# Causal masking on GpSimd instead of TensorE, the second softmax division on GpSimd, and a few instructions issued at other places

## The chip, the cores and the metric

The program runs on 1 core of one Trainium2 chip, in one launch. The metric is the device time in microseconds (us), the median of several runs: 1357.43 us for the kernel before (3 runs, 1357.02 to 1357.74). The engines of the core are TensorE (PE in the profile), VectorE (DVE), ScalarE (ACT), GpSimd (POOL) and SyncE (SP), each of which works through its own list of instructions in order; they wait for one another on semaphores.

## The reference

A trunk of two layers works on 512 tokens of 1024 features in float32, with 16 heads of 64 features.

```
layer 0:  hn = rms_norm(h) * g;  q, k, v = hn @ W_qkv
          z = q.k / 8 ;  strict: key < query
          w = sigmoid(z) * prod over later keys of (1 - sigmoid(z))     # stick-breaking weights
layer 1:  k, v, f from rms_norm(h) @ W_kvf, q from rms_norm(h) @ W_q;  k, q with a norm per head
          z = q.k / 8 + F[query] - F[key],  F = cumsum(log_sigmoid(f + b))
          w = softmax(z) over key <= query                              # forgetting attention
each:     h += (w @ v) @ W_o
          h += (silu(hn2 @ W_g) * (hn2 @ W_u)) @ W_d                    # 22 tiles of 128 hidden features
          h += sigmoid(rms_norm(h) @ W_gate) * (p[layer] @ W_proj)
```

## The kernel before, in words

Everything lies transposed: features on the 128 partitions, the 512 tokens as columns. So h is eight tiles h[0..7] of 128x512, and a norm's factor per token has to be spread over the partitions: `norm_spread` (L255 on) does it with four small matmuls of plain float32 (L258), and ScalarE copies the result `rb` to SBUF.

Each float32 operand of a product is split into a high part in the type fp32r and a low remainder, and a product is three matmuls: high by high, high by low, low by high (`mm3`, L274 to L276; `by_token`, L431 to L434, for q, k and v). The weights come in "units" of 128x1024 by DMA on SP's queue. ScalarE rounds a unit to its high part `wh` (L154 for the first units, L171 and L175 later), and VectorE subtracts to get `wl` (L139).

The attention of a layer goes head by head. `qk` makes the projections of two heads; `expand` and `put` turn them into `qd`, `kd` and `ke` (kd and ke exchange halves by DMAs on GpSimd's queue, L561). `front(hd)` has three score tiles, each in a PSUM bank `z`: tile 0 holds the block j=0 of 128 tokens against 512 columns, tile 1 the block j=1 against 384, tile 2 the block j=3 against 128 and the block j=2 against 256. `scores` issues two matmuls for a block (L635 with ke, L636 with kd). For block j=3 before computes 256 columns and uses the last 128 of them. In layer 1 `hide` then adds a mask to the diagonal block of 128 columns by a third matmul (L643) with `identb` and a bfloat16 mask; in tile 2 one such matmul of 256 columns serves both blocks. In layer 0 the sigmoids are computed with no mask and GpSimd's affine_select (L680) sets the forbidden weights to zero.

After the scores, layer 1 does for each tile: VectorE adds the head's row of gate sums `gb` (brought from DRAM by a GpSimd DMA, L656) and takes the minimum in one instruction (L695), ScalarE takes the exponential with the sum beside it (L699), VectorE the reciprocal (L701), and ScalarE multiplies the weights by it (L703). Layer 0 uses sigmoids (L677), a scan (L684) and a multiplication (L687).

`back(hd)` turns the weights on TensorE (transposes, L736, into `pt`), ScalarE and VectorE split them (L737, L139), and TensorE multiplies them with v (L744). After the second head of a pair, at L764 to L772, VectorE and ScalarE make from the result the operands `bh` and `bl` of the output projection.

What stands between these steps on TensorE is a pump (`Filler`, table `STEPS`): matmuls of later projections, of later v, and in the end of `first_part` (eight tiles of the first half of W_o, 12 matmuls each) are handed out in small numbers between the steps of the heads, so that TensorE has work while a head's weights are computed on the other engines. Behind the last head the second half of W_o follows; three of its tiles are begun (9 matmuls each) before the ones that need the last pair of heads. A scheduler places the instructions at build time and so fixes each engine's list; `pin` forces a given order there.

The end of the kernel is the gate of layer 1: per tile VectorE computes `s` (L359), adds it to h (L360) and SP stores h (L362).

Of the kernel before, what the change touches and what calls it, by code (L numbers as in the profile page):

```python
# [24 lines left out]
P = 128  # L25
# [19 lines left out]
I32 = mybir.dt.int32  # L45
BF16 = mybir.dt.bfloat16

# [38 lines left out]
def trunk(ctx, tc, xT, pT, small, wf, wall, out, dump=None):  # L86
# [29 lines left out]
    make_identity(nc, ident)  # L116


    identb = const.tile([P, P], BF16, name="identb")
    nc.vector.tensor_copy(identb, ident)  # L120
    masks = []
    for i, (op, fill) in enumerate(((ALU.is_gt, -1.0e30), (ALU.is_ge, 1.0e30))):
        mf = tp.tile([P, S], F32, name="mf", tag="ta")
        nc.gpsimd.memset(mf[:, :P], 0.0)
        nc.gpsimd.affine_select(out=mf[:, :P], in_=mf[:, :P], pattern=[[1, P]], compare_op=op,
                                fill=fill, base=0, channel_multiplier=-1)
        mb = const.tile([P, P], BF16, name=f"mask{i}")
        nc.vector.tensor_copy(mb, mf[:, :P])
        masks.append(mb)
    one = const.tile([P, 1], F32, name="one")  # L130
# [16 lines left out]
    def load_half(u, i):  # L147

        if i == 0:
            units[u] = tuple(wpool.tile([P, 1024], F32R, name=f"w{x}{u}", tag=f"w{x}", bufs=WBUFS)  # L150
                             for x in "hl")
        wh, wl = units[u]
        c = slice(i * 512, i * 512 + 512)
        nc.scalar.copy(wh[:, c], raws[u][:, c])  # L154
        minus(wl[:, c], raws[u][:, c], wh[:, c])
        if i == 1:
            raws.pop(u)
            state["unit"] = u + 1
# [59 lines left out]
    def add_square(k, c0=0, cn=S):  # L218
        c = slice(c0, c0 + cn)
        if k == 0:  # L220
            nc.scalar.activation(acc[:, c], h[k][:, c], AF.Square)
        else:
            sq = tp.tile([P, S], F32, name="sq", tag="ta")
            nc.scalar.activation(sq[:, :cn], h[k][:, c], AF.Square)
            nc.vector.tensor_tensor(acc[:, c], acc[:, c], sq[:, :cn], ALU.add)
# [45 lines left out]

    def mm3(ps, wblk, xh, xl, first, last):
        wh, wl = wblk
        nc.tensor.matmul(ps, wh, xh, start=first, stop=False)  # L274
        nc.tensor.matmul(ps, wh, xl, start=False, stop=False)  # L275
        nc.tensor.matmul(ps, wl, xh, start=False, stop=last)  # L276
# [21 lines left out]
    def ffn(layer, buf, g_next):  # L298
        last = layer == 1
        with tc.tile_pool(name=f"pf{layer}", bufs=8, space=PSUM, reuse_waits="tile") as ppool["d"], \  # L300
# [54 lines left out]
            def close_gate(n, s, pp):  # L355
                cn = S // len(pp)
                for c0, ps in pp:
                    c = slice(c0, c0 + cn)
                    nc.vector.tensor_tensor(s[:, c], s[:, c], ps[:, :cn], ALU.mult)  # L359
                    nc.vector.tensor_tensor(h[n][:, c], h[n][:, c], s[:, c], ALU.add)  # L360
                    if last:
                        nc.sync.dma_start(out[:, n * S + c0:n * S + c0 + cn], h[n][:, c])  # L362
                    else:
                        emit_x(n, 1 - buf, g_next, True, c0, cn)
# [33 lines left out]
    def attention(layer, buf):  # L398
        stick = layer == 0
        mask = masks[layer]  # L400
        xs = operand(buf)
        with tc.tile_pool(name=f"pa{layer}", bufs=1, space=PSUM, reuse_waits="tile") as pa, \
# [67 lines left out]
            if stick:  # L470
# [10 lines left out]
                run(v0)  # L481
                rb = norm_spread(r, pz, "z")
            oh, ol = bh[1 - buf], bl[1 - buf]
# [146 lines left out]

            def scores(zt, c, n, d, j, s0, first=True, done=stick):
# [4 lines left out]
                nc.tensor.matmul(zt[:, c:c + n], qd[:, t], kd[:, s0:s0 + n], start=False, stop=done)  # L636

            def hide(zd):

                if stick:  # L640
                    return
                m = mask.unsqueeze(1).to_broadcast([P, zd.shape[1] // P, P])
                nc.tensor.matmul(zd, identb, m, start=False, stop=True)  # L643


# [4 lines left out]
            def front(hd):  # L650
# [3 lines left out]
                if not stick:  # L654
                    gb = a2.tile([P, S], F32, name="gb", tag="gb")
                    nc.gpsimd.dma_start(gb, gdram[hd:hd + 1, :].to_broadcast([P, S]))  # L656
                for ti, segs in enumerate(TILES):
                    n = sum(sg[2] for sg in segs)
                    z = pz.tile([P, S], F32, name="z", tag="z")
                    if ti == 2:  # L660

                        scores(z, 0, 256, d, 3, 256, True, False)
                        scores(z, 256, 256, d, 2, 256, False)
                        z = z[:, P:]
                        hide(z[:, :2 * P])
                    else:
                        scores(z, 0, n, d, segs[0][0], segs[0][0] * P)
                        z = z[:, :n]
                        hide(z[:, :P])
                    w = a2.tile([P, S], F32, name="w", tag="w", bufs=WB[layer])  # L670
# [18 lines left out]
                    else:  # L689
# [4 lines left out]
                        for si, (j, c, m) in enumerate(segs):  # L694
                            nc.vector.tensor_tensor_reduce(  # L695
                                w[:, c:c + m], z[:, c:c + m], gb[:, j * P:], 1.0, 3.0e38,
                                ALU.add, ALU.min, mx[:, si:si + 1])
# [15 lines left out]
            def back(hd):  # L713
# [26 lines left out]
                def product(gi, low):  # L740
                    blks, th, tl, uses = groups[gi]
                    for s, c, m in uses:
                        vv = v[:, s, hd % 4].rearrange("p a d -> p (a d)")
                        nc.tensor.matmul(po[:, :m], vv, (tl if low else th)[:, c:c + m],  # L744
                                         start=gi == 0 and not low, stop=gi == 2 and low)

# [30 lines left out]
            if stick:  # L777
                run(qk(0))
            else:
# [12 lines left out]
                run(group(0, sums, spread))  # L792
                gdram = tok["g"]
                run(expand(0))
            for e in attn_order(layer)[2:]:
                i = int(e[1:])
                if e == "e7":
                    continue
                fill.add(e, qk(i) if e[0] == "p" else expand(i) if e[0] == "e" else
                         group(i) if e[0] == "g" else values(i, (bank("v"),) if i == 0 else ()))  # L800
# [212 lines left out]
```

## Time and profile before

| | |
|---|---|
| median of 3 runs | 1357.43 us (1357.02 to 1357.74) |
| the profiled execution | 1356.89 us |
| its span, in which the rows stand | 1355.2 us |
| TensorE busy | 1337.9 us (99%), 6236 matmuls |
| VectorE busy | 808.2 us (60%) |
| ScalarE busy | 628.0 us (46%) |
| GpSimd busy | 75.5 us (6%) |
| chain that ended last | 86% on TensorE |

All times in rows are microseconds from the start of the span, unless marked ns. A row of a timeline has the start, the duration, the engine, the line of the kernel, the operation, and output<-inputs with their shapes; in brackets stands how long the engine was idle before it and what ended that. Matmuls overlap in the array: a row's duration is from its issue to its end, and what a matmul costs in a dense stretch is the distance from its start to the next one's, not its duration. PEld is TensorE's weight load, which runs beside the matmul ahead of it.

### The profile page before, as it was taken

How to read it: one execution, taken by the hardware profiler on the slowest of the kernel's cores; microseconds unless marked ns; L12 is line 12 of the kernel's file. 1: busy time of each engine (PE TensorE's matmuls, PEld its weight loads, DVE VectorE, ACT ScalarE, POOL GpSimd, SP SyncE). 2: the span in 40 equal slices, each digit the busy share in tenths (PEclk: the TensorE clock that was granted, in tenths of full speed). 3: DMA queues.
4: the chain of work that ended last, by engine and by line, in shares of the span. 5: the costliest groups of instructions: out<-in, count | busy, mean ns of one | idle time of the engine just before them, and what ended most of it. 6: DMA issues, size and time to landing. Idle time of an engine off the chain costs nothing.

```text
span 1355.2 us, 16550 instructions
## 1 busy us (share of the span) xinstructions
PE 1337.9 (99%) x6236; PEld 1095.2 (81%) x6236; DVE 808.2 (60%) x1388; ACT 628.0 (46%) x1099; POOL 75.5 (6%) x146
## 2 busy tenths in 40 slices
PE   8999999999999999999999999999999999999998
PEld 7788887888888888888877777777888888888887
DVE  6898998754444443334867887787544444434335
ACT  6676776532223332222648788685322322322212
POOL 0221220000000000000010101000000000000000
PEclk9999999999999999999999999999999999999999
DMA  6332331233333233322333433332333323322323
GB/s 203 109 94 63 101 99 66 93 101 94 95 104 96 93 94 100 102 94 70 111 110 94 110 101 102 101 99 81 101 96 105 95 93 95 107 93 94 95 68 109
DMA packets 41856, 133.34 MB, mean 98 GB/s; under 512 B 7456, under 2 KB 7840, under 8 KB 41776
## 3 DMA queue, kind: packets, MB, share of 16 engines
q1 hardware_dynamic: 37248, 119.63, 28.2%
q0 software_dynamic: 4384, 12.62, 3.6%
q8 instruction: 49, 0.80, 0.3%
q14 instruction: 31, 0.25, 0.1%
q10 hardware_dynamic: 144, 0.03, 0.0%
HBM read 121.73 MB, written 2.14 MB: 91 GB/s over the span
## 4 chain that ended last, share of the span: by engine, by line
PE 86%; ACT 4%; issue 4%; DVE 3%; DMA 1%; POOL 1%; SPq 0%; POOLq 0%; DVEq 0%; ACTq 0%
PE ps L275 24%; PE ps L276 24%; PE ps L274 24%; PE pb L431 2%; PE pb L434 2%; PE pb L433 2%; PE po L744 2%; PE pt L736 2%; PE z L635 1%; PE z L636 1%; ACT wh L171 1%; POOL w L680 1%; ACT w L699 1%; DMA raw<-in_w_dram 0%; ACT ke L549 0%
## 5 line engine op out<-in xcount | busy, mean ns | idle before, releaser
L274 PE MATMUL ps<-bh,wh 128*128 128x512 f32 x1216 | 478.1, 394 | 1.9 <-DVE bh L767 1.9
L275 PE MATMUL ps<-bl,wh 128*128 128x512 f32 x1216 | 474.8, 390 | 1.0 <-DVE bl L139 1.0
L276 PE MATMUL ps<-bh,wl 128*128 128x512 f32 x1216 | 474.9, 391 | 0.0
L175 ACT CAST wh<-raw 128x1024 fp32r<-128x1024 f32 x188 | 197.7, 1052 | 484.5 <-PE ps L275 426.0
L139 DVE TENSOR_TENSOR wl<-raw,wh 128x1024 fp32r<-128x1024 f32 (+1 forms) x196 | 235.1, 1200 | 162.9 <-ACT wh L175 161.8
L276 PEld LDWEIGHTS ps<-bh,wl 128*128 128x128 f32 x1216 | 228.3, 188 | 47.7 <-DVE wl L139 0.4
L274 PEld LDWEIGHTS ps<-bh,wh 128*128 128x128 f32 x1216 | 228.3, 188 | 47.1 <-DVE bh L767 2.5
L275 PEld LDWEIGHTS ps<-bl,wh 128*128 128x128 f32 x1216 | 228.5, 188 | 46.2 <-DVE bl L139 2.0
L431 PE MATMUL pb<-wh,bh 128*128 128x512 f32 x256 | 105.8, 413 | 1.9 <-ACT wh L154 1.3
L317 DVE TENSOR_TENSOR s<-s,ps 128x512 f32<-128x512 f32 x44 | 30.2, 687 | 126.9 <-PE ps L276 126.7
L433 PE MATMUL pb<-wl,bh 128*128 128x512 f32 x256 | 101.3, 396 | 0.2 <-DVE wl L139 0.2
L434 PE MATMUL pb<-wh,bl 128*128 128x512 f32 x256 | 100.7, 396 | 0.0
L315 DVE TENSOR_TENSOR s<-ps,rb 128x512 f32<-128x512 f32 x44 | 30.2, 690 | 95.7 <-PE ps L276 79.9
L274 PE MATMUL ps<-eh,wh 128*128 128x512 f32 x224 | 87.2, 389 | 0.0
L276 PE MATMUL ps<-eh,wl 128*128 128x512 f32 x224 | 87.2, 389 | 0.0
L275 PE MATMUL ps<-el,wh 128*128 128x512 f32 x224 | 87.1, 389 | 0.0
L431 PEld LDWEIGHTS pb<-wh,bh 128*128 128x128 f32 x256 | 48.4, 189 | 10.4 <-issue 2.1
L434 PEld LDWEIGHTS pb<-wh,bl 128*128 128x128 f32 x256 | 48.1, 188 | 9.7
L433 PEld LDWEIGHTS pb<-wl,bh 128*128 128x128 f32 x256 | 48.5, 190 | 7.3 <-DVE wl L139 0.5
L736 PE MATMUL pt<-ident,w 128*128 128x128 f32 x320 | 52.9, 273 | 1.3 <-DVE w3l L139 1.3
L684 DVE TENSOR_TENSOR_SCAN e<-e,own 128x512 f32<-128x512 f32 (+1 forms) x64 | 51.5, 826 | 3.1 <-ACT e L677 2.8
L736 PEld LDWEIGHTS pt<-ident,w 128*128 128x128 f32 x320 | 39.7, 140 | 13.2 <-DVE w3l L139 3.1
(177 smaller groups left out, 1572.0 us busy)
## 6 DMA issues: line engine op xcount, KB each, us to landing
raw<-in_w_dram SPq DMA_DIRECT2D x212, 512.0 KB, 3.5
kd<-ke POOLq DMA_DIRECT2D x32, 128.0 KB, 3.3
ke<-kd POOLq DMA_DIRECT2D x32, 128.0 KB, 3.7
gb<-gdram POOLq DMA_DIRECT2D x16, 256.0 KB, 3.5
h<-in_x_dram SPq DMA_DIRECT2D x8, 256.0 KB, 4.4
raw<-in_w_dram SPq DMA_DIRECT2D x8, 256.0 KB, 4.0
out_dram<-h SPq DMA_DIRECT2D x7, 256.0 KB, 2.1
pf<-in_p_dram SPq DMA_DIRECT2D x2, 512.0 KB, 4.6
```

The lines of the kernel that those rows point to most:

```text
L139: nc.vector.tensor_tensor(out, a, b.bitcast(F32), ALU.subtract)
L175: nc.scalar.copy(wh, raw)
L274: nc.tensor.matmul(ps, wh, xh, start=first, stop=False)
L275: nc.tensor.matmul(ps, wh, xl, start=False, stop=False)
L276: nc.tensor.matmul(ps, wl, xh, start=False, stop=last)
L315: nc.vector.tensor_tensor(s, g, rb, ALU.mult)
L317: nc.vector.tensor_tensor(s, s, u, ALU.mult)
L431: pin(nc.tensor.matmul(ps, xh, wh, start=k == 0, stop=False), stick and k == 0)
L433: nc.tensor.matmul(ps, xh, wl, start=False, stop=False)
L434: nc.tensor.matmul(ps, xl, wh, start=False, stop=k == ND - 1)
L684: nc.vector.tensor_tensor_scan(e[:, c:c + m], e[:, c:c + m], own[:, :m], 1.0, ALU.mult, ALU.max)
L736: nc.tensor.transpose(pt[:, bi * P:(bi + 1) * P], blk(j, s), ident)
```

## The change

1. The masks: `identb`, the two mask tiles and `hide`'s matmul go (48 matmuls in layer 1). Instead `gb` gets 128 more columns, and GpSimd writes a large number over the forbidden part of its diagonal block, four affine_selects of 128x128 a head: for block 0 and block 3 (into the added columns) when `gb` has landed, for blocks 1 and 2 when the row has been used by the tile before.
2. The scores of block j=3 are computed with 128 columns, not 256: 64 matmuls in both layers.
3. The multiplication by the reciprocal in layer 1 goes from ScalarE (L703) to GpSimd (64 instructions).
4. `first_part` keeps back its eighth tile; its 12 matmuls come behind the last head's last product and ahead of the late part, in both layers.
5. Order: in layer 0 `norm_spread` comes five steps later in `qk(0)`; the first weight unit's copy comes ahead of the square of h[0] on ScalarE; in layer 1 the first steps of `values(0)` are called before `expand(0)`.
6. In the last gate one residual addition (tile 6) goes from VectorE to GpSimd.

```
-    identb = const.tile([P, P], BF16, name="identb")
...
-        nc.scalar.copy(wh[:, c], raws[u][:, c])
+        pin(nc.scalar.copy(wh[:, c], raws[u][:, c]), u == 0)
...
-            nc.scalar.activation(acc[:, c], h[k][:, c], AF.Square)
+            pin(nc.scalar.activation(acc[:, c], h[k][:, c], AF.Square), True)
...
-                    nc.vector.tensor_tensor(h[n][:, c], h[n][:, c], s[:, c], ALU.add)
+                    eng = nc.gpsimd if last and n == ND - 2 else nc.vector
+                    eng.tensor_tensor(h[n][:, c], h[n][:, c], s[:, c], ALU.add)
...
-                rb = norm_spread(r, pz, "z")
...
-            def hide(zd):
-                if stick:
-                    return
-                m = mask.unsqueeze(1).to_broadcast([P, zd.shape[1] // P, P])
-                nc.tensor.matmul(zd, identb, m, start=False, stop=True)
...
+                    gb = a2.tile([P, S + P], F32, name="gb", tag="gb")
+                    nc.gpsimd.dma_start(gb[:, :S], gdram[hd:hd + 1, :].to_broadcast([P, S]))
+                    def hide(o, i):
+                        nc.gpsimd.affine_select(out=gb[:, o * P:o * P + P], in_=gb[:, i * P:i * P + P],
+                                                pattern=[[1, P]], compare_op=ALU.is_ge, fill=1.0e30,
+                                                base=0, channel_multiplier=-1)
+                    hide(0, 0)
+                    hide(4, 3)
...
-                    if ti == 2:
-                        scores(z, 0, 256, d, 3, 256, True, False)
-                        scores(z, 256, 256, d, 2, 256, False)
-                        z = z[:, P:]
-                        hide(z[:, :2 * P])
-                    else:
-                        scores(z, 0, n, d, segs[0][0], segs[0][0] * P)
-                        z = z[:, :n]
-                        hide(z[:, :P])
+                    for j, c, m in segs:
+                        scores(z, c, m, d, j, j * P, c == 0, c + m == n)
...
+                        if ti < 2:
+                            hide(ti + 1, ti + 1)
...
-                            nc.scalar.activation(w[:, c:c + m], w[:, c:c + m], AF.Copy,
-                                                 scale=mx[:, 2 + si:3 + si])
+                            nc.gpsimd.tensor_scalar_mul(w[:, c:c + m], w[:, c:c + m],
+                                                        mx[:, 2 + si:3 + si])
...
-                run(qk(0))
+                q0 = qk(0)
+                for _ in range(5):
+                    next(q0)
+                rb = norm_spread(r, pz, "z")
+                run(q0)
...
-                for n in range(ND):
+                for n in range(ND - 1):
...
+            ps, b = bank("z")(), take(WO_SPLIT)
+            for i, (xh, xl) in enumerate(operand(1 - buf, range(WO_SPLIT))):
+                mm3(ps, block(b + i), xh, xl, i == 0, i == WO_SPLIT - 1, i == 0)
+            grow(ND - 1, ps)
```

In the changed kernel the line numbers are lower: L635/L636 become L621/L622, L736 and L744 become L720 and L728, L274 to L276 become L260 to L262, the DMAs of L561 and L656 become L547 and L637, the division is L687 and the new select is L640.

GpSimd's list in layer 1, early heads, before. `gb` is the row of gate sums, kd and ke are the expanded keys; all its instructions here are DMA issues.

```order
L656 DMA gb<-gdram 128x512 x3
L561 DMA kd<-ke 64x512 x2
L561 DMA ke<-kd 64x512 x2
L656 DMA gb<-gdram 128x512 x2
L561 DMA kd<-ke 64x512 x2
```

The same place of the changed kernel, where `w` are the weights and `mx` holds the reciprocals:

```order
L687 TENSOR_SCALAR w<-w,mx 128x512
L640 AFFINE_SELECT gb<-gb 128x128 x2
L687 TENSOR_SCALAR w<-w,mx 128x384
L637 DMA gb<-gdram 128x512
L687 TENSOR_SCALAR w<-w,mx 128x128
L687 TENSOR_SCALAR w<-w,mx 128x256
L640 AFFINE_SELECT gb<-gb 128x128 x3
```

The multiplications and selects of several heads now stand in one list with the DMA issues of L637 and L547, and each comes up only when those ahead of it are done.

TensorE in the last head of layer 1, before, from the last score product's mask to the transposes of the same tile (`z` the scores, `pt` the transposes, `po` the products with v, `ps` the filler from `first_part`):

```order
L736 MATMUL pt<-ident,w 128x128
L274 MATMUL ps<-bh_107,wh_7647 128x512
L275 MATMUL ps<-bl_109,wh_7647 128x512
L276 MATMUL ps<-bh_107,wl_7648 128x512
L274 MATMUL ps<-bh_107,wh_7647 128x512
L275 MATMUL ps<-bl_109,wh_7647 128x512
L744 MATMUL po<-w1h,v 128x256
L744 MATMUL po<-w2l,v 128x384
L744 MATMUL po<-w2l,v 128x256
L744 MATMUL po<-w1l,v 128x256
L736 MATMUL pt<-ident,w 128x128 x6
```

TensorE at this place in the changed kernel, from the last two score products on:

```order
L621 MATMUL z<-ke,qd 128x256
L622 MATMUL z<-kd,qd 128x256
L728 MATMUL po<-w3h,v 128x512
L720 MATMUL pt<-ident,w 128x128 x2
L728 MATMUL po<-w2h,v 128x384
L728 MATMUL po<-w2h,v 128x256
L728 MATMUL po<-w3l,v 128x512
L728 MATMUL po<-w1h,v 128x256
L728 MATMUL po<-w2l,v 128x384
L728 MATMUL po<-w2l,v 128x256
L720 MATMUL pt<-ident,w 128x128 x2
L260 MATMUL ps<-bh_91,wh_7758 128x512
```

Before, eight filler matmuls, eight products and four transposes stand between the mask and the six transposes (nine of these rows are above the ones shown); in the changed kernel the six come as two and then four, and between the scores and the four stand three filler matmuls (one shown), eight products (seven shown) and six transposes.

TensorE at the end of the last head of layer 1, before (bh and bl under this number are the attention's output, the wh after it the weights of W_o):

```order
L744 MATMUL po<-w1l,v 128x256
L274 MATMUL ps<-bh_107,wh_7647 128x512 x2
L274 MATMUL ps<-bh_107,wh_7739 128x512
L275 MATMUL ps<-bl_109,wh_7647 128x512
L276 MATMUL ps<-bh_107,wl_7648 128x512
```

And in the changed kernel, where `pb` is the kept-back tile:

```order
L728 MATMUL po<-w1l,v 128x256
L260 MATMUL pb<-bh_91,wh_7654 128x512
L261 MATMUL pb<-bl_93,wh_7654 128x512
L262 MATMUL pb<-bh_91,wl_7655 128x512
L260 MATMUL pb<-bh_91,wh_7654 128x512
```

The 12 matmuls of the kept-back tile (the first five of them above) now stand between the last product with v and the first matmul that needs the last pair of heads.

## Rows read from the trace of the kernel before

**Rows 1.** The page's part 1: busy time, share of the span, matmuls.
```profile
PE 1337.9 (99%) x6236; PEld 1095.2 (81%) x6236; DVE 808.2 (60%) x1388; ACT 628.0 (46%) x1099; POOL 75.5 (6%) x146
```

**Rows 2.** Windows, layer 1's attention: length, busy us of each engine, clock, DMA.
```profile
700.00:920.00 220.00, 215.66 (x1121) 167.96 (x1120) 172.32 (x454) 172.61 (x413) 26.07 (x49) 1.00 0.35 101
```

**Rows 3.** TensorE's waits: total us, times, longest.
```profile
PE ps L274 <- DVE bh L767: 1.9, 2, 1.4
...
PE ps L275 <- DVE bl L139: 1.0, 2, 0.5
```

**Rows 4.** Timeline of TensorE around a mask of 128 columns, layer 1.
```profile
791.37 0.23 PE L643 MATMUL z<-mask,identb 128*128 128x128 bf16 x1
...
791.72 0.40 PE L433 MATMUL pb<-wl,bh 128*128 128x512 f32 x1
791.95 0.39 PE L434 MATMUL pb<-wh,bl 128*128 128x512 f32 x1
```

**Rows 5.** Timeline of TensorE around a mask of 256 columns.
```profile
784.18 0.28 PE L635 MATMUL z<-ke,qd 128*128 128x256 f32 x1
...
784.43 0.28 PE L643 MATMUL z<-mask,identb 128*128 128x256 bf16 x1
...
784.79 0.39 PE L433 MATMUL pb<-wl,bh 128*128 128x512 f32 x1
```

**Rows 6.** Timeline: plain float32 matmuls of 128 columns (four in the program).
```profile
690.01 1.05 PE L258 MATMUL pb<-ident,r 128*128 128x128 f32 x8
690.82 0.48 PE L431 MATMUL pb<-wh,bh 128*128 128x512 f32 x1
```

**Rows 7.** Timeline of the start: ScalarE and TensorE.
```profile
4.97 0.61 ACT L221 ACTIVATE acc<-h 128x512 f32<-128x512 f32 x1
...
6.14 0.50 PE L431 MATMUL pb<-wh,bh 128*128 128x512 f32 x1 [1.26 <-ACT wh L154]
...
30.70 1.16 PE L258 MATMUL pb<-ident,r 128*128 128x128 f32 x8 [1.06 <-DVE r L237]
```

**Rows 8.** Timeline: the end of layer 1's attention on TensorE.
```profile
916.37 0.31 PE L744 MATMUL po<-w1l,v 128*128 128x256 f32 x1
918.07 0.96 PE L274 MATMUL ps<-bh,wh 128*128 128x512 f32 x3 [1.39 <-DVE bh L767]
919.51 0.50 PE L275 MATMUL ps<-bl,wh 128*128 128x512 f32 x1 [0.49 <-DVE bl L139]
```

**Rows 9.** Timeline, last head of layer 1: from scores to transposes.
```profile
908.28 0.28 PE L643 MATMUL z<-mask,identb 128*128 128x256 bf16 x1
...
911.20 0.80 ACT L703 ACTIVATE w<-w,mx 128x128 f32<-128x128 f32 x2
...
912.00 0.83 PE L736 MATMUL pt<-ident,w 128*128 128x128 f32 x6
...
912.58 0.48 PE L276 MATMUL ps<-bh,wl 128*128 128x512 f32 x1
```

**Rows 10.** Timeline, an earlier head of layer 1: division and transposes.
```profile
800.78 0.50 ACT L703 ACTIVATE w<-w,mx 128x256 f32<-128x256 f32 x1
...
801.31 0.49 PE L736 MATMUL pt<-ident,w 128*128 128x128 f32 x3
```

**Rows 11.** Groups by form on POOL.
```profile
L680 POOL TENSOR_SCALAR_AFFINE_SELECT w<-w 128x128 f32<-128x128 f32 x32 | 21.4, 672 | 68.4 <-ACT w L677 66.6 <-PE pt L736 1.7
...
L125 POOL TENSOR_SCALAR_AFFINE_SELECT mf<-mf 128x128 f32<-128x128 f32 x2 | 0.6, 282 | 0.0
...
L487 POOL MEMSET own<- 128x512 f32 x1 | 0.5, 514 | 0.0
```

**Rows 12.** Timeline, layer 0: a select beside VectorE's scan.
```profile
73.70 1.82 POOL L680 TENSOR_SCALAR_AFFINE_SELECT w<-w 128x128 f32<-128x128 f32 x1 [0.91 <-ACT w L677]
...
74.22 1.21 DVE L684 TENSOR_TENSOR_SCAN e<-e,own 128x512 f32<-128x512 f32 x1
```

**Rows 13.** Timeline of the end: the last full additions to h.
```profile
1350.31 1.02 DVE L360 TENSOR_TENSOR h<-h,s 128x512 f32<-128x512 f32 x2
```

More of the change, by code (lines that the diff above doesn't have):

```diff
@@ L45 @@
 I32 = mybir.dt.int32
-BF16 = mybir.dt.bfloat16
 def run(steps):
@@ L116, in trunk @@
     make_identity(nc, ident)
-    identb = const.tile([P, P], BF16, name="identb")
[L120 to L129, printed above, removed]
     one = const.tile([P, 1], F32, name="one")
@@ L270, in norm_bounce, with mm3 @@
         return rb
-    def mm3(ps, wblk, xh, xl, first, last):
+    def mm3(ps, wblk, xh, xl, first, last, ordered=False):
         wh, wl = wblk
-        nc.tensor.matmul(ps, wh, xh, start=first, stop=False)
+        pin(nc.tensor.matmul(ps, wh, xh, start=first, stop=False), ordered)
         nc.tensor.matmul(ps, wh, xl, start=False, stop=False)
@@ L399, in attention @@
         stick = layer == 0
-        mask = masks[layer]
         xs = operand(buf)
@@ L629, in expand, with scores @@
                 yield from put(p, turned("q"), gq8, turned("k"), sm[:, C_KG:C_KG + 1])
-            def scores(zt, c, n, d, j, s0, first=True, done=stick):
+            def scores(zt, c, n, d, j, s0, first, last):
                 qd, kd, ke = d
@@ L635, in scores @@
                 nc.tensor.matmul(zt[:, c:c + n], qd[:, t], ke[:, s0:s0 + n], start=first, stop=False)
-                nc.tensor.matmul(zt[:, c:c + n], qd[:, t], kd[:, s0:s0 + n], start=False, stop=done)
-            def hide(zd):
-                if stick:
-                    return
-                m = mask.unsqueeze(1).to_broadcast([P, zd.shape[1] // P, P])
-                nc.tensor.matmul(zd, identb, m, start=False, stop=True)
+                nc.tensor.matmul(zt[:, c:c + n], qd[:, t], kd[:, s0:s0 + n], start=False, stop=last)
             TILES = [[(0, 0, 512)], [(1, 0, 384)], [(3, 0, 128), (2, 128, 256)]]
@@ L654, in front @@
                 if not stick:
-                    gb = a2.tile([P, S], F32, name="gb", tag="gb")
-                    nc.gpsimd.dma_start(gb, gdram[hd:hd + 1, :].to_broadcast([P, S]))
+                    gb = a2.tile([P, S + P], F32, name="gb", tag="gb")
[6 more added lines that the diff above has]
+                    hide(4, 3)
                 for ti, segs in enumerate(TILES):
@@ L695, in front @@
                             nc.vector.tensor_tensor_reduce(
-                                w[:, c:c + m], z[:, c:c + m], gb[:, j * P:], 1.0, 3.0e38,
+                                w[:, c:c + m], z[:, c:c + m],
+                                gb[:, S:] if j == 3 else gb[:, j * P:S], 1.0, 3.0e38,
                                 ALU.add, ALU.min, mx[:, si:si + 1])
+                        if ti < 2:
+                            hide(ti + 1, ti + 1)
                         for si, (j, c, m) in enumerate(segs):
@@ L743, in product @@
                         vv = v[:, s, hd % 4].rearrange("p a d -> p (a d)")
-                        nc.tensor.matmul(po[:, :m], vv, (tl if low else th)[:, c:c + m],
-                                         start=gi == 0 and not low, stop=gi == 2 and low)
+                        pin(nc.tensor.matmul(po[:, :m], vv, (tl if low else th)[:, c:c + m],
+                                             start=gi == 0 and not low, stop=gi == 2 and low),
+                            hd == NH - 1 and gi == 2 and low)
                 turn(0)
@@ L793, in attention @@
                 gdram = tok["g"]
+                v0 = values(0, (bank("v"),))
+                for _ in range(4):
+                    next(v0)
                 run(expand(0))
@@ L799, in attention @@
                 fill.add(e, qk(i) if e[0] == "p" else expand(i) if e[0] == "e" else
-                         group(i) if e[0] == "g" else values(i, (bank("v"),) if i == 0 else ()))
+                         group(i) if e[0] == "g" else v0 if i == 0 else values(i))
             def first_part():
-                for n in range(ND):
+                for n in range(ND - 1):
                     ps = yield from dense_steps(take(WO_SPLIT), operand(1 - buf, range(WO_SPLIT)))
```

## The prediction

> **What bounds the kernel now.** I read the page's part 1 first: TensorE is busy 1337.9 of 1355.2 us [rows 1], so a change pays where it takes columns from TensorE or ends one of its few stops, 17.3 us in all. The windows by stage come next: in layer 1's attention (700 to 920 us) TensorE is busy 215.66 of 220.0 us, VectorE 172.32, ScalarE 172.61 and GpSimd 26.07 [rows 2]. So ScalarE and VectorE stand at 78% there, GpSimd at 12%, and TensorE's stops are 4.3 us. Then TensorE's waits show what ends the stops: at the end of both attentions it waits for the last pair of heads, twice for bh (1.9 us, the longer 1.4) and twice for bl (1.0 us) [rows 3]. Last the timelines, for the distance from one matmul's start to the next one's, which is what a matmul costs in a dense stretch.
>
> **The change part by part.** The profiled execution took 1356.89 us, the span 1355.2 and 1.7 around it; it lies 0.54 under the median of 1357.43. The sum is made against 1356.89.
>
> *Mask matmuls.* A matmul of 512 columns keeps its distance of 0.23 us (791.72 to 791.95). From a mask of 128 columns at 791.37 to the second matmul behind it at 791.72 are 0.35 us, in which one of 512 columns has its 0.23, so the mask costs 0.12 [rows 4]. In the same way the mask of 256 columns costs 784.79 - 784.43 - 0.23 = 0.13 [rows 5]. With 16 heads, two masks of 128 and one of 256 each: 32 x 0.12 + 16 x 0.13 = 5.9 us off, all on the path, since TensorE is dense there.
>
> *Scores of 128 columns.* Two score matmuls of 256 columns take 0.25 us (784.18 to 784.43), 0.125 each [rows 5]. No row has a matmul of 128 columns in fp32r, so bounds: by columns, on the line through 512 (0.23) and 256 (0.125), it would be about 0.07, which saves 64 x 0.055 = 3.5 us. The nearest rows of that width are of two kinds. The mask costs 0.12, though its columns should take 0.07: the load of the next weights finds no cover behind so short a matmul. The plain float32 ones of L258, four in the program, which the trace shows as eight, take 0.81 us from their start to the next matmul's and 1.05 to their own end, so 0.20 to 0.26 each [rows 6]; that would add 64 x 0.075 = 4.8 to 64 x 0.135 = 8.6. Transposes of 128 columns, a third kind, come at 0.58 / 6 = 0.10 [rows 9]. I take the mask's 0.12, thus no change, because each score matmul loads weights of its own, as the mask's neighbours do.
>
> The Trainium skill ("TensorE: Matmul & The Clock Gate", section "Back-to-back issue gap") gives a sustained spacing of about 81 ns for pairs of weight load and matmul at 128 columns. By that the 64 would save an estimated 64 x 0.044 = 2.8 us and the sum would be lower by as much; the mask's 0.12 here does not agree, and no run here shows a stream of such matmuls.
>
> *The start.* TensorE stops 1.06 us at L258, for a factor whose work on VectorE is late [rows 7]; 15 matmuls of 0.23 us now stand ahead of it, so the stop goes: -1.1. The first projection waits 1.26 us for the copy of the first weights, ahead of which ScalarE squares h[0] from 4.97 on for 0.61 [rows 7]. That square goes behind; the weights' own arrival and VectorE's high-low step bound what is won: between 0 and -0.5, and I take -0.3. The early steps of values(0) leave TensorE's order as it was up to the first scores: 0.
>
> *The kept-back tile.* 12 matmuls x 0.23 = 2.8 us now stand where TensorE waits at the end of each attention. In layer 1 the last product starts at 916.37, bh comes at 918.07 and bl at 919.51 [rows 8]; the cover reaches from about 916.6 to 919.4, with the nine matmuls that follow it the waits of 1.39 and 0.49 go, together -1.9. In layer 0 the two others (0.5 and 0.5) go too: -1.0 [rows 3].
>
> *What it takes away.* Those 12 matmuls, and the masks, were also filler. In layer 1's last head 3.6 us pass from the end of tile 2's scores (908.4) to its transposes at 912.00, with the division's 0.80 just ahead [rows 9]; TensorE's work between filled that. In the changed order I count work by these distances: 2.6 us between the scores of tile 2 and the transposes that need them, for the last head, 2.7 and 2.8 for the two before; tile 1 has under 3 twice. The chain (minimum, exponentials, reciprocal, division) took no less than 3.3 (an estimate: 3.6 less some 0.3 of foreign work on ScalarE). So three times about 0.6 and twice 0.3: +2.4, and a little less in layer 0, whose heads are covered by layer 0's longer order, put at nothing.
>
> *Division and selects on GpSimd.* ScalarE loses 64 instructions: the two of a tile 2 take 0.80 [rows 9], the one of 256 columns 0.50 [rows 10], and the two wider tiles at least 0.50 each, so 16 x 1.8 = 29 us or more of its 172.61 [rows 2]; that makes its casts and exponentials come sooner. GpSimd gets 64 multiplications and 64 selects. Bounds for one multiplication: a memset of 512 columns takes 0.514, an undisturbed select of 128 takes 0.282, a select in layer 0 0.672 in the mean [rows 11], and one beside VectorE's scan 1.82 [rows 12]. Undisturbed, GpSimd does a tile as fast as ScalarE; at 0.672 a piece, tile 2's two divisions (0.80 on ScalarE) take 1.34 and come 0.5 late. In an ordinary head the division ends at 801.28 and the transposes begin at 801.31 [rows 10]: there is no slack, so a late division is paid. Against it stands ScalarE's relief, a sixth of its queue. I take +1.0 in sum; the ends are -1.5 (relief only) and 16 x 0.5 = +8.
>
> Queued behind a multiplication in GpSimd's list are the selects, the gb DMA and the kd/ke exchange of later heads; the exchange is needed a pair of heads later, so I cost it at nothing; if that cover is gone it is in the +8.
>
> *The last gate.* One addition of 1.02 / 2 = 0.5 us goes from VectorE to GpSimd [rows 13]; it shares the end with the DMA behind it. Between -0.5 and +0.6; I take 0.
>
> Sum: -5.9 + 0 - 1.4 + 0 - 2.9 + 2.4 + 1.0 + 0 = -6.8, so 1350.1 against the profiled execution and, with the 0.54, about 1350.5 for the median.
>
> **The rivals.** *A*, the forecast. *B*: the 128-column scores run as the plain float32 ones. For it: L258's are the only 128-column products with float32 operands in these rows that are no transposes [rows 6]; against it: the transposes at 0.10 [rows 9]. Price +4.8 to +8.6, in the middle +6.7, time about 1357.
>
> *C*, the other side: GpSimd's list becomes what TensorE waits for. A select or multiplication meets a two-input VectorE instruction and stands still as in layer 0, where 1.82 is needed for what takes 0.28 alone [rows 11, 12]; the reciprocal's division comes behind selects of the next head, and the turns stop, in each of 16 heads at two tiles. With 0.672 - 0.282 = 0.39 late at each of the two, 16 x 2 x 0.39 = 12.5 in place of the 1.0, so about 1362. It decides from 0.6 us a head over the forecast (9.6 us): below that the kernel is not slower by what can be told. For it: no slack at 801.31. Against it: GpSimd is 12% busy, VectorE's minimum takes z from PSUM and so has one operand in SBUF, and ScalarE's relief runs against it.
>
> The Trainium skill ("SBUF — State Buffer", section "Who interferes with whom") says that GpSimd and VectorE share a pair of ports under a lock which one instruction holds to its end, and that a VectorE instruction with two SBUF inputs contends with a GpSimd one that reads SBUF. The 1.82 beside the scan agrees with it; by this rule the splits from PSUM would leave GpSimd alone, and wl = raw - wh (both in SBUF) would hold up a division.
>
> *D*: the kept-back tile only moves the stop: the last heads of both layers lack all of the filler, 2 x 2.8 = 5.6 in place of the 2.4: -6.8 + 3.2 = -3.6, about 1353.8. It lies in the forecast's own range. That an edit does nothing is seen for values(0) already.
>
> **How the numbers follow.** What a measurement of this kernel can tell from no change is about 0.2%, 2.7 us: faster is under 1354.7, slower over 1360.1. A with D has 0.60, with its own range of 1345.0 (3.5 from narrower scores, 1.5 from ScalarE) to 1354.5. B has 0.20, mostly within 0.2%; C 0.12, with smaller delays partly in "same"; B and C together 0.08, slower. The range reaches from 1345.0 to 1358.0 and leaves out C and the worst of B. Chances: faster 0.62 (A and the mildest of B), same 0.20, slower 0.18.
>
> **What would show it.** In the profile of the changed kernel: the distance of the 128-column scores (0.12 by A, 0.20 to 0.26 by B); the stops at the end of both attentions gone, with new ones ahead of the transposes of heads 13 to 15 (about 2 us); the wait at L258 gone; divisions on GpSimd of 0.3 to 0.7 us, by C over 1 us, with TensorE's transposes waiting for POOL in all heads. Wrong it is if TensorE's busy time falls by less than 4 us, or if its idle time grows past 20.

## The result, and the profile after

The changed kernel is slower: 1367.99 us (median of 4 runs, 1366.67 to 1368.67) against 1357.44; the ratio is 1.0074, 95% interval 1.0062 to 1.0085, which is 10 us. The prediction said 1350.5 and a range to 1358.0. The profiled execution took 1368.35, its span 1366.6.

First the page's part 1, as in [rows 1]:

```profile
PE 1337.8 (98%) x6188; PEld 1096.3 (80%) x6188; DVE 811.1 (59%) x1384; ACT 601.5 (44%) x1035; POOL 168.8 (12%) x271
```

48 matmuls fewer, and the same busy time. By stretches it fell by 5.5 us in layer 1's attention and by 2.7 in layer 0's, and rose by 2.1 and 3.3 behind them, where the kept-back tiles (2.7 us each) went, and by 2.6 in the start, whose first matmuls ran slowly (below). TensorE's idle time grew from 17.3 us to 28.8, and GpSimd's busy time from 75.5 to 168.8. So both signs came that the prediction had named for being wrong: a busy time that falls by less than 4 us, and an idle time past 20. The span is longer by 11.4 us. Starts of the same matmuls in both traces say where (the spread is `norm_spread`'s first matmul):

| stretch | forecast | measured |
|---|---|---|
| start to the first score of layer 0 | -1.4 | +0.25 |
| from there to layer 1's first spread | -1.0 | -0.9 |
| from there to layer 1's first score | 0 | +0.1 |
| layer 1, first score to last product with v | -5.2 | +6.95 |
| from there to the last matmul | +0.8 | +1.5 |
| last matmul to the end of the span | 0 | +3.6 |

(The forecast's column puts the kept-back 12 matmuls, 2.7 us, where they went: out of the attention and into what follows.) Two stretches make the result: layer 1's attention and the very end. A second profile of the same changed kernel (e16_after_again, below) differs from this one by 0.1 or less in these two, but by 1.9 in the first stretch and 1.7 in the fifth, so the other rows are not told from chance.

**Layer 1's attention.** Windows of this stretch, first score to last product, of the kernel before and of the changed one (length, busy us of PE, PEld, DVE, ACT, POOL, clock, DMA):

```profile
710.76:916.37 205.61, 204.42 (x1072) 160.00 (x1072) 163.76 (x437) 168.04 (x404) 22.36 (x42) 1.00 0.35 101
```

```profile
710.18:922.74 212.56, 198.90 (x1005) 155.46 (x1006) 164.11 (x435) 140.36 (x339) 114.45 (x166) 1.00 0.33 95
```

TensorE's work fell by 5.5 us, of which 2.7 are the 12 matmuls that were kept back, and its idle time rose from 1.2 to 13.7. TensorE's waits in the changed kernel (total us, times, longest) say for whom:

```profile
PE pt L720 <- POOL w L687: 9.9, 11, 1.8
PE z L621 <- DVE mx L676: 2.5, 4, 1.6
```

The transposes wait for the division on GpSimd. Seven of these eleven waits, 6.2 of the 9.9 us, end after 890 us, in the last heads, from which the kept-back tile had taken filler. What one division takes is in the groups by form (count, busy us, mean ns, idle before), first GpSimd's in the changed kernel, then ScalarE's in the kernel before:

```profile
L687 POOL TENSOR_SCALAR w<-w,mx 128x512 f32<-128x512 f32 x16 | 26.5, 1655 | 6.9 <-DVE mx L685 4.2 <-ACT w2h L721 1.3 <-PE pt L720 0.9
...
L687 POOL TENSOR_SCALAR w<-w,mx 128x384 f32<-128x384 f32 x16 | 20.6, 1286 | 8.5 <-DVE mx L685 5.2 <-PE pb L421 1.6 <-DVE mm L582 1.1
...
L687 POOL TENSOR_SCALAR w<-w,mx 128x256 f32<-128x256 f32 x16 | 15.2, 947 | 0.0
L687 POOL TENSOR_SCALAR w<-w,mx 128x128 f32<-128x128 f32 x16 | 10.9, 681 | 6.3 <-DVE mx L685 4.3 <-PE po L728 0.8 <-PE pb L420 0.5
```

```profile
L703 ACT ACTIVATE w<-w,mx 128x512 f32<-128x512 f32 x16 | 11.5, 718 | 0.3 <-DVE mx L701 0.2
L703 ACT ACTIVATE w<-w,mx 128x384 f32<-128x384 f32 x16 | 9.8, 613 | 1.7 <-DVE mx L701 1.7
L703 ACT ACTIVATE w<-w,mx 128x256 f32<-128x256 f32 x16 | 8.0, 497 | 0.0
L703 ACT ACTIVATE w<-w,mx 128x128 f32<-128x128 f32 x16 | 6.4, 398 | 1.8 <-DVE mx L701 1.8
```

Per head that is 4.57 us on GpSimd against 2.23 on ScalarE. It is nearly all GpSimd's own pace and little disturbance: of the 14 multiplications of 512 columns that stand alone in the timeline, 12 took 1.56 or 1.57 us, and two were drawn out. One of each kind:

```profile
887.75 2.38 POOL L687 TENSOR_SCALAR w<-w,mx 128x512 f32<-128x512 f32 x1 [0.49 <-PE z L622]
...
897.17 1.56 POOL L687 TENSOR_SCALAR w<-w,mx 128x512 f32<-128x512 f32 x1
```

What a wait looks like, in the timeline of VectorE's reciprocals, GpSimd and TensorE:

```profile
780.96 0.17 DVE L685 RECIPROCAL mx<-mx 128x2 f32<-128x2 f32 x1
...
781.15 0.72 POOL L640 TENSOR_SCALAR_AFFINE_SELECT gb<-gb 128x128 f32<-128x128 f32 x1
...
781.87 1.50 POOL L687 TENSOR_SCALAR w<-w,mx 128x128 f32<-128x128 f32 x2
...
783.42 0.44 PE L720 MATMUL pt<-ident,w 128*128 128x128 f32 x2 [1.73 <-POOL w L687]
```

The reciprocals are there at 781.13, a select stands ahead until 781.87, both divisions take to 783.37, and TensorE starts 0.05 later. On ScalarE the two divisions of such a tile took 0.80 [rows 9]. The select ahead is this tile's own case; in the mean the list adds little (e12_div_tt, below).

**The end.** The last matmul starts 4.9 us before the end of the span in the kernel before and 8.5 in the changed one. Timeline of the changed kernel's end:

```profile
1357.88 1.27 POOL L348 TENSOR_TENSOR h<-h,s 128x512 f32<-128x512 f32 x1 [439.20 <-DVE s L345]
...
1358.15 0.28 PE L262 MATMUL ps<-ph,wl 128*128 128x256 f32 x1
1358.28 1.16 DVE L348 TENSOR_TENSOR h<-h,s 128x256 f32<-128x256 f32 x1
...
1359.80 0.42 DVE L348 TENSOR_TENSOR h<-h,s 128x256 f32<-128x256 f32 x1
```

VectorE is done at 1360.22 and the span ends at 1366.6. The events of the closing sequence of each program (engine, operation, count, shortest/median/longest ns, first and last start) name what lies between, first of the changed kernel, then of the kernel before:

```profile
L1006 POOLq DRAIN  x3: 40/102/8021, 1357.8 to 1366.4; - x3
```

```profile
L1007 POOLq DRAIN  x3: 40/93/7262, 896.8 to 1354.9; - x3
```

DRAIN is an instruction of the closing sequence. The row of GpSimd's long one begins while GpSimd's last instruction still runs, and ends 6.7 us after the end of that one. Before, that was from 896.8 to 904.0, behind GpSimd's last DMA issue, and nobody saw it. With the addition on GpSimd, which ended at 1359.15, it was from 1357.8 to 1365.9.

**Scores and start.** The score matmuls of tile 2 in the changed kernel (timeline of TensorE):

```profile
897.92 0.22 PE L621 MATMUL z<-ke,qd 128*128 128x128 f32 x1
897.98 0.28 PE L622 MATMUL z<-kd,qd 128*128 128x128 f32 x1
898.09 0.33 PE L621 MATMUL z<-ke,qd 128*128 128x256 f32 x1
898.26 0.28 PE L622 MATMUL z<-kd,qd 128*128 128x256 f32 x1
898.38 0.38 PE L720 MATMUL pt<-ident,w 128*128 128x128 f32 x2
```

0.46 us from the first score to the transposes. In the kernel before the four of 256 columns take 0.47, in the median of the tiles in layer 0 behind which a dense matmul follows. With the narrow ones the distances are 0.06, 0.11 and then 0.17 for 256 columns (these are the medians over the program's tiles too): what the columns save is lost on the matmuls behind. The start of TensorE's work:

```profile
6.79 0.63 PE L421 MATMUL pb<-wh,bl 128*128 128x512 f32 x1
7.21 0.63 PE L418 MATMUL pb<-wh,bh 128*128 128x512 f32 x1
7.64 0.63 PE L420 MATMUL pb<-wl,bh 128*128 128x512 f32 x1
```

The first projection starts 0.8 earlier than in [rows 7], but until about 11 us these matmuls are 0.43 apart and not 0.23.

### The profile page after: what moved, and what is told of

It is laid out like the page before. It is cut to its first block, busy times and chain, and to the rows that moved or that the text cites. A ratio compares the mean times of both kernels' runs of the same rounds, so it can differ in the third digit from the quotient of the medians.

```text
span 1366.6 us, 16653 instructions
## 1 busy us (share of the span) xinstructions
PE 1337.8 (98%) x6188; PEld 1096.3 (80%) x6188; DVE 811.1 (59%) x1384; ACT 601.5 (44%) x1035; POOL 168.8 (12%) x271
## 4 chain that ended last, share of the span: by engine, by line
PE 84%; issue 5%; DVE 4%; ACT 3%; POOL 2%; DMA 1%; SPq 0%; POOLq 0%; DVEq 0%; ACTq 0%
PE ps L260 23%; PE ps L261 23%; PE ps L262 23%; PE pb L420 3%; PE pb L418 3%; PE pb L421 3%; PE po L728 2%; PE pt L720 1%; POOL w L687 1%; PE z L621 1%; PE z L622 1%; DMA raw<-in_w_dram 1%; DVE w L676 1%; POOL w L661 1%; DVE wl L158 1%
## 5 line engine op out<-in xcount | busy, mean ns | idle before, releaser
L260 PE MATMUL ps<-bh,wh 128*128 128x512 f32 x1208 | 474.9, 393 | 0.0
L262 PE MATMUL ps<-bh,wl 128*128 128x512 f32 x1208 | 471.4, 390 | 0.0
L262 PEld LDWEIGHTS ps<-bh,wl 128*128 128x128 f32 x1208 | 226.8, 188 | 47.8 <-DVE wl L125 0.4
L260 PEld LDWEIGHTS ps<-bh,wh 128*128 128x128 f32 x1208 | 227.0, 188 | 43.9 <-DVE h L281 0.4
L260 PE MATMUL ps<-eh,wh 128*128 128x512 f32 x224 | 87.1, 389 | 0.0
L262 PE MATMUL ps<-eh,wl 128*128 128x512 f32 x224 | 87.1, 389 | 0.0
L687 POOL TENSOR_SCALAR w<-w,mx 128x512 f32<-128x512 f32 (+1 forms) x64 | 72.9, 1142 | 21.7 <-DVE mx L685 13.7
L720 PE MATMUL pt<-ident,w 128*128 128x128 f32 x320 | 53.7, 275 | 11.4 <-POOL w L687 9.9
L720 PEld LDWEIGHTS pt<-ident,w 128*128 128x128 f32 x320 | 39.7, 140 | 27.4 <-POOL w L687 14.4
```

The costliest lines, as they stand in the source:

```text
L260: pin(nc.tensor.matmul(ps, wh, xh, start=first, stop=False), ordered)
L687: nc.gpsimd.tensor_scalar_mul(w[:, c:c + m], w[:, c:c + m], mx[:, 2 + si:3 + si])
L720: nc.tensor.transpose(pt[:, bi * P:(bi + 1) * P], blk(j, s), ident)
```

## The experiments

Each ratio is to runs of the kernel before on the same chip; 0.001 is 1.36 us. Beside the experiments the kernel before took 1359.6 to 1360.3, so ratios are compared and not times.

**e1_div_act, e2_add_dve, e3_both: undo the division, the last addition, both.**

```
-  nc.gpsimd.tensor_scalar_mul(w[:, c:c + m], w[:, c:c + m], mx[:, 2 + si:3 + si])
+  nc.scalar.activation(w[:, c:c + m], w[:, c:c + m], AF.Copy, scale=mx[:, 2 + si:3 + si])   # e1, e3
...
-  eng = nc.gpsimd if last and n == ND - 2 else nc.vector
+  eng = nc.vector                                                                           # e2, e3
```

> The changed kernel with the division back on ScalarE, all else kept. Theory 1 (GpSimd's own pace at a multiplication by a column, 1.57 us for 512 columns against 0.72 on ScalarE, makes the weights late): the waits of transposes for GpSimd (9.9 us) and those that follow from them go, the time falls by 10 to 13 us, to 1355 to 1358 us. Theory 2 (the filler taken away and the selects of the masks make the heads late, whoever divides): it falls by at most 3 us, to about 1365.

> The changed kernel with the last gate's addition back on VectorE, all else kept. Theory 1 (GpSimd's drain at the end of the program takes some 7 us from its last instruction and was hidden as long as GpSimd stopped at 897 us): the time from VectorE's last instruction to the end falls from 6.4 to about 3.1, the whole by 3 to 3.7 us, to about 1364.6. Theory 2 (the last 3.3 us are a late DMA or chance): it stays at 1368, or moves by the 0.3 that the addition itself cost.

> The changed kernel with both undone: mask selects, narrow scores, kept-back tile and early orders stay. If the two costs add: 1352 to 1354, faster than before by 3.5 to 5 us. If the filler that was taken away is what counts: 1360 or more.

| | ratio | 95% interval | against the changed kernel |
|---|---|---|---|
| changed kernel | 1.0074 | 1.0062 to 1.0085 | |
| e1_div_act | 1.0000 | 0.9991 to 1.0010 | -10.0 us |
| e2_add_dve | 1.0054 | 1.0039 to 1.0069 | -2.7 us |
| e3_both | 0.9968 | 0.9956 to 0.9979 | -14.4 us |

In e1 and e2 the first theory holds each time, and the costs add (10.0 + 2.7 = 12.7 against 14.4, within the intervals). Windows of layer 1's attention in e3_both:

```profile
709.31:912.87 203.56, 199.59 (x1012) 156.95 (x1012) 161.29 (x434) 167.68 (x403) 42.48 (x102) 1.00 0.35 99
```

TensorE's work is the changed kernel's within 0.7 us, its idle time 4.0 and not 13.7. So the division alone cost 9 to 10 us there. In e2 the drain began at 919.1, the last wait of SP for the others' closing was 0.5 as before, not 3.5, and the last matmul starts 4.9 us before the end, as before.

**e4_before_div: only the division moved, in the kernel before.**

> The kernel before with the division alone moved to GpSimd (masks stay matmuls). Theory 1 (pace): 8 to 12 us slower than before, 1365 to 1369, with transposes waiting for GpSimd. Theory 2 (selects and missing filler): within 3 us of before, since neither is there.

Ratio 1.0048 (1.0031 to 1.0065): 6.5 us slower, under the expected 8 to 12 but far from the other theory's 3. The waits of transposes for GpSimd are 5.7 us here, 9.9 in the changed kernel: which fits that with masks and filler in place TensorE covers some of the longer chain.

**e12_div_tt: the same division in a faster form.**

```
-  nc.gpsimd.tensor_scalar_mul(w[:, c:c + m], w[:, c:c + m], mx[:, 2 + si:3 + si])
+  nc.gpsimd.tensor_tensor(w[:, c:c + m], w[:, c:c + m],
+                          mx[:, 2 + si:3 + si].to_broadcast([P, m]), ALU.mult)
```

> The changed kernel with GpSimd's multiplication as a two-input instruction, the reciprocal spread over the columns, in place of the one by a column scalar; the list and the places stay. Theory 1 (the pace of that one instruction decides): if 512 columns take 1.27 us, as the two-input addition at the end did, in place of 1.57, the waits for GpSimd fall from 9.9 to 5 to 7 us and the whole by 2 to 5 us against the changed kernel. Theory 2 (GpSimd's place in the chain, its list and the hops decide): within 1.5 us of the changed kernel whatever its pace.

Groups by form on GpSimd in e12, and TensorE's wait for it:

```profile
L687 POOL TENSOR_TENSOR w<-w,mx 128x512 f32<-128x512 f32 x16 | 17.6, 1100 | 6.5 <-DVE mx L685 3.9 <-ACT w2h L721 1.2 <-PE pt L720 0.8
```

```profile
PE pt L720 <- POOL w L687: 5.6, 9, 1.3
```

1.10 us in place of 1.66, with list and places kept, and the waits fall from 9.9 to 5.6; ratio 1.0049 (1.0031 to 1.0067), 3.4 us faster than the changed kernel, with some 3 us of uncertainty. In the profiles layer 1's attention is 4.1 us shorter than in the changed kernel, where e1's is 10.1 shorter. So the pace of that one instruction counts, as theory 1 had it; its four multiplications still take 3.1 us a head against ScalarE's 2.2, and why this rest is so dear no run separates. The place in GpSimd's list is hardly the cause: from the end of a reciprocal to the start of its division a head's three tiles wait 1.40 us together in the changed kernel and 1.28 in e1, where ScalarE divides, while the divisions themselves take 4.56 and 2.13.

**e6_before_memset: a GpSimd instruction at the end, with no data in common with it.**

```
+  if last and n == ND - 2:
+      nc.gpsimd.memset(s[:, 0:1], 0.0)
```

> The kernel before with one addition: a memset of one column on GpSimd behind the last gate's tile 6, into a tile that nobody reads any more. It shares no data with the end. Theory 1 (GpSimd's drain at the end of the program lasts about 7 us from its last instruction): the end comes 2.5 to 3.5 us later, as with the addition on GpSimd. Theory 2 (the addition's hold on VectorE, or its DMA, made the end late): no change.

Ratio 1.0024 (1.0014 to 1.0035), 3.3 us slower, for a memset of 0.10 us. The drain in its closing sequence:

```profile
L1009 POOLq DRAIN  x3: 40/93/6816, 1356.5 to 1363.8; - x3
```

Theory 1 holds: in the five profiles whose last GpSimd instruction is late (the changed kernel, e1, e6, e12, e16) the program ends 7.5 us after the end of that instruction, and the last matmul starts 8.4 or 8.5 us before the end; in the other twelve it starts 4.9 before it. So a late GpSimd instruction costs this kernel 3.5 to 3.6 us.

**e7_no_kept, e8_mask_mm, e9_wide, e10_div_dve: the other parts, each undone or changed in e3_both.** e7 lets `first_part` make all eight tiles and has no kept-back one; e8 adds the masks in layer 1 by a matmul per tile and has no selects; e9 has

```
+  if ti == 2:
+      scores(z, 0, 256, d, 3, 256, True, False)
+      scores(z, 256, 256, d, 2, 256, False, True)
+      z = z[:, P:]
...
```

and e10 divides with `nc.vector.tensor_scalar_mul`.

> The version e3_both (division on ScalarE, last addition on VectorE) without the kept-back tile: first_part makes all eight tiles again. Theory 1 (the filler taken from the last heads is worth what the tile covers at the end): within 1 us of e3_both. Theory 2 (the prediction: 2.9 won at the two ends, 2.4 given back): 0.5 to 1 us slower than e3_both. Theory 3 (the kept-back tile is a full gain): 2.5 to 3 us slower.

> e3_both with the masks of layer 1 as matmuls again (48 of them, in bfloat16), the rest of e3_both kept. Theory 1 (the prediction): 5.9 us slower than e3_both, 1361. Theory 2 (GpSimd's selects stand before the kd/ke exchange and the gate rows in its list and give back half and more): 1 to 3 us slower than e3_both.

> e3_both with 256 columns again for the scores of block j=3 (64 matmuls). Theory 1 (the prediction: the weight load of the next one finds no cover, so a matmul of 128 columns costs what one of 256 does): within 1 us of e3_both. Theory 2 (by columns): 3.5 us slower. Theory 3 (128 columns run at a quarter of the pace): 5 to 8 us faster.

> e3_both with the division of layer 1 on VectorE instead of ScalarE. If the tail from the reciprocal (VectorE) to the transposes decides, one hop less and a faster multiplication make it 1 to 4 us faster than e3_both; if VectorE's own list (78% busy in the stage) decides, it is as much slower.

| | ratio | 95% interval | against e3_both (0.9968) |
|---|---|---|---|
| e7_no_kept | 0.9982 | 0.9973 to 0.9992 | +1.9 us |
| e8_mask_mm | 0.9996 | 0.9987 to 1.0005 | +3.8 us |
| e9_wide | 0.9958 | 0.9945 to 0.9972 | -1.4 us |
| e10_div_dve | 0.9966 | 0.9954 to 0.9979 | -0.3 us |

Each difference carries about 2 us of uncertainty. e7 lies between its theories 2 and 3: the tile seems to be worth something, about 2 us, but with that uncertainty it is hardly told from nothing. The profiled execution of e7 was the fastest of its ten (1355.09 against a median of 1358.44), so its stretches need not be the median's. Its waits for the last heads are back, as in [rows 3]:

```profile
PE ps L260 <- DVE bh L752: 1.6, 2, 1.4
...
PE ps L261 <- DVE bl L125: 1.0, 2, 0.5
```

In layer 1 its stretch from the last product to the first low-part matmul is as long as before (3.1 us), while e3's attention without those 12 matmuls is only 0.1 us shorter than e7's: there the tile's 2.7 us were nearly all needed as filler. In e8 the mask matmuls cost 3.8 us, not 5.9, which is between its two theories; in layer 1's attention TensorE works 5.0 us more than in e3 (204.6 against 199.6) and idles 1.9 us less (2.0 against 4.0). In e9 narrow scores are no gain that can be told. In e10 a division of 512 columns takes 0.49 us on VectorE, and the kernel is neither faster nor slower by it.

**e15_no_mask: e9_wide without the selects (layer 1 then has no causal mask).**

> The version e9_wide without its 64 selects: layer 1 has no causal mask at all, so this part of the computation is left out. Against e9_wide it shows what GpSimd's selects cost. Theory 1 (selects in GpSimd's list, ahead of the exchange of kd and ke, give back half of what the mask matmuls cost): 2 to 3 us faster than e9_wide. Theory 2 (the selects are hidden, and with TensorE's work shortened the chain over the other engines binds): within 1 us of e9_wide.

Ratio 0.9955 (0.9940 to 0.9970) against 0.9958: theory 2. GpSimd's selects are hidden within what can be told, about 3 us; nothing shows that the part that the masks' removal did not bring is lost on them. In layer 1's attention TensorE still waits for DMA-fed keys, for ScalarE's casts and for the split weights, mostly a few tenths at a time; that this chain now binds is likely, but not shown by an experiment.

**e13_wide_dve, e14_wide_warm, e14b_wide_warm, e16_after_again.** e13 is e9 with the division on VectorE, e14 is e9 with `WARM = 19` in place of 16, run twice, and e16 is the changed kernel again.

> The version e9_wide with the division on VectorE. Both edits alone were at or ahead of e3_both: if they add, 1 to 3 us faster than e9_wide; if VectorE's list is the bound by then, the same as e9_wide.

> The version e9_wide with 19 warm-up transposes at the start instead of 16. In some profiles the granted clock of TensorE rose to its full level at about 7 us, in others at 11, and the first stretch was 1.7 us longer there. If the gap between the warm-up and the first projection decides, the clock is full from about 7 us on; if it is chance, or the clock's rise is bound to something else, no difference.

> e14_wide_warm a second time, beside the changed kernel on the same chip: 1.0 to 1.2% faster than the changed kernel and 0.4 to 0.5% faster than the kernel before; the granted clock of TensorE full from about 7 us on if the longer warm-up holds it, from 11 us in half of the cases if not.

> The changed kernel a second time, beside the others on the same chip: 0.7% slower than the kernel before; the granted clock at the start either way.

e13: 0.9969 (0.9959 to 0.9980), so the two do not add; it is e3's ratio. e14: 0.9954 (0.9938 to 0.9970) and 0.9957 (0.9941 to 0.9974); e16: 1.0085 (1.0070 to 1.0100). So masks by selects, kept-back tile, early orders and the division left on ScalarE make the kernel 0.45% faster than before (6 us) and 1.3% faster than the changed one. The longer warm-up shows no difference to e9. In e16 the first matmuls are 0.23 apart from 7 us on, as in [rows 4], with the very program that had 0.43 above; of 17 profiles 6 show the slow start, one of them in e6_before_memset, whose start is the kernel before's. So the slow start is not made by the change. The first score of layer 0 comes 1.9 us earlier in e16's profile than in the first one.

## Why the prediction was wrong

**The step that failed** is the price of the division on GpSimd: "Undisturbed, GpSimd does a tile as fast as ScalarE", and from it +1.0 with an upper end of +8. The rows used for its price were a memset of 512 columns (0.514) and a select of 128 (0.282) [rows 11]. Neither is a multiplication by a column scalar. Measured, that takes 1.66 for 512 columns and 0.68 for 128 in the mean, against 0.718 and 0.398 on ScalarE, 2.3 us more a head, and it stands on a chain that [rows 10] had shown to have no slack. The term is 9 to 10 us (e1, e3), with the filler of the kernel before still 6.5 (e4), and even the upper end fell short. Both bounds had been taken from instructions that read one operand or none and do no arithmetic by a scalar; a bound from rows of another kind was no bound.

**Rival C had the side, the place and nearly the size, and the wrong cause.** It had 0.12. It let GpSimd be held up by two-input VectorE instructions or by its list. Such holding up occurs: at the end VectorE's addition of 256 columns took 1.16 us beside GpSimd's and 0.42 right after, and two multiplications of 14 were drawn out to 2.17 and 2.38, both beside two-input instructions of VectorE. The Trainium skill ("SBUF — State Buffer", section "Who interferes with whom") has a VectorE instruction with two SBUF inputs contend with a GpSimd instruction that reads SBUF, and these rows agree. But 12 of 14 ran at their own pace, the list held a head's divisions up by 0.12 us more than ScalarE's does, TensorE waited 11 times and not at two tiles of every head, and e12, which changes only the form and so the pace of that instruction, wins 3.4 us. The argument against C, "GpSimd is 12% busy", was an average and said nothing of a chain with no slack.

**The last gate** was put at 0, between -0.5 and +0.6, as the price of an addition. It cost 2.7 (e2) and, with a memset of 0.10 us in its place, 3.3 (e6); at the end of the profiles it is 3.5 to 3.6 each time. That GpSimd had its last instruction at 897 us, and so drained in the shade, was in the trace of before, and no part of the working looked at it.

**The masks**: 5.9 forecast, 3.8 measured (e8), with selects that cost nothing that can be told (e15). The distances in [rows 4, 5] were read rightly; the time that TensorE saved there (5.0 by e8) was in part waited for elsewhere (1.9), of which the prediction's +2.4 spoke, in the last heads only.

**The narrow scores**: 0 forecast, and 0.46 us for a tile's four against 0.47. The single distances were not the 0.12 of the forecast, but 0.06 and 0.11 with 0.17 behind; that their sum is the same was not foreseen. Rival B (plain float32's pace) is out: no distance reached 0.20.

**The kept-back tile**: -2.9 and +2.4, so 0.5 net; 1.9 measured, with 2 of uncertainty. That the waits at both ends would go was right, and that layer 1 would give most of it back too.

**The start**: the stop at L258 went, and in the profiles with a quick start the first score of layer 0 comes 1.0 to 1.8 us earlier (-1.4 forecast; 0.7 in e14, with its longer warm-up). In the profiled run of the changed kernel the slow first matmuls took that back.

Without the division and the addition the forecast's own terms give -6.8 - 1.0 = -7.8 us; e3 measured -4.3, e9 -5.7. (A slip beside it: 1356.89 - 6.8 + 0.54 is 1350.6, not 1350.5.)

## What to carry to other kernels

Price an instruction on an engine by a row of the same form on that engine; where there is none, the price is open upward, and a chain with no slack is no place for it. An engine's low busy share is no cover for work that stands between two others. And look where each engine has its last instruction: if its closing takes long, one more instruction near the end moves the end of the program.

## What the runs showed of the hardware

- GpSimd's drain at the end of the program ended 6.7 to 7.0 us after the end of GpSimd's last instruction in all 17 profiles, and it lengthened the program only where that instruction was late.
- On GpSimd a multiplication by a column scalar (1.56 or 1.57 us for 128x512 float32 in 12 of 14) is slower than the same as a two-input instruction with the scalar spread over the columns (1.04 or 1.05 in 14 of 16, in e12_div_tt). In the mean VectorE takes 0.49 (e10_div_dve) and ScalarE 0.72.
- Of two 128-column matmuls ahead of two of 256 columns the first takes 0.06 us to the next start and the second 0.11, and the 256-column one that follows then 0.17 and not 0.12.
- In 6 of 17 profiles the first projections run 0.43 us apart until about 10 to 11 us, in the others 0.23 from 7 us on, with the same program (the changed kernel and e16_after_again); the warm-up transposes end by 5.2 us in both. The clock column stands at 1.00 there in both. Matmuls of 512 columns are 0.43 us apart also where that column shows 0.50, the lower of TensorE's two levels (1.2 GHz), in the window below; so the level at the start is read from the distance.
- In four profiles the granted clock fell to 0.50 for 3.4 us in mid-program (e2 at 727.8, e6 at 922.0, e9 at 910.5, e14b at 909.4 us), each time after stops of TensorE. In e2 such a stop lasted 1.92 us; in the changed kernel one of 1.60 us at the same place was followed by no fall, and its attention in layer 1 took 1.9 us less. The window of e2's fall (length, busy us of PE, PEld, DVE, ACT, POOL, clock, DMA):

```profile
727.80:731.20 3.40, 3.40 (x10) 2.60 (x9) 2.77 (x5) 2.28 (x5) 3.10 (x4) 0.50 0.40 100
```
